# Two 128x512 elementwise steps of a quartered feed-forward pass, put on VectorE in place of GpSimd

## The chip, the cores and the metric

The kernel runs on one core of one Trainium2 chip. The metric is the device time of one launch in microseconds; of the kernel before there are three runs and one profiled execution. The core has five engines with a queue of their own each, taken in order: TensorE (PE in the profile, with its weight loads as PEld), VectorE (DVE), ScalarE (ACT), GpSimd (POOL) and SyncE (SP). Transfers are issued from such queues and then run on the DMA engines beside them.

## The reference

A bidirectional encoder of two layers on one sequence of 512 positions with 1024 features. Each layer is a half-step feed-forward, a mix of three kinds of attention, a second half-step feed-forward, and an embedding term that is gated. What matters here is the feed-forward, which stands four times in the program:

```
def swiglu(x, w_gate, w_up, w_down):
    return (jax.nn.silu(x @ w_gate) * (x @ w_up)) @ w_down
...
        h = h + 0.5 * swiglu(rms_norm(h, ffn1_norm[i]), ffn1_w_gate[i], ffn1_w_up[i], ffn1_w_down[i])
...
        h = h + 0.5 * swiglu(rms_norm(h, ffn2_norm[i]), ffn2_w_gate[i], ffn2_w_up[i], ffn2_w_down[i])
```

The inner width is 2816, so the gate and up products have 22 tiles of 128 columns each. All data is 32-bit float.

## The kernel before, in words

**Precision and passes.** Each operand of a matmul is split in a part hi of fewer bits (a cast on ScalarE, L101 for weights, L235 for data) and a rest lo (a subtraction on VectorE, L107 and L236). Each product runs in three passes on TensorE: hi by hi, lo by hi, hi by lo (mm3, L226 to L229, all recorded under L224). The weights are split in blocks of 1024 or, in the pass below, of 512 columns; at most two blocks ahead of the product that uses them, into three buffers of whi and wlo. Data is kept transposed, 128 features by 512 positions a tile.

**The stages.** The trace calls the four feed-forwards ffn10 (first one, layer 0), ffn20 (second one, layer 0), ffn11 and ffn21. In each, the 22 tiles go in 11 pairs. Pairs 0 and 1 are plain. Pairs 2 to 10 go in quarters: two halves of the features (z0 to z3 and z4 to z7) by the two tiles of the pair, over two halves A and B of the positions, with seven products of 128x256 instead of eight (class Quad, L462). One quad stands for the gate (g2 to g10), one for the up side (u2 to u10). A product is four mm3, so twelve matmuls with 256 columns. Products 1, 2, 5, 6, 3 and 7 of a pair's two quads come in turn, the gate's before the up's; product 4 is put off to the next pair, behind its products 1 and 2. After pairs 1, 3, 5, 7 and at the end stand groups of the down product (down_part, L546), whose results VectorE adds to h at L554; that frees their bank of the accumulator memory.

**A quad's operands.** Quad.load (L474) takes three tiles of raw weights, X and Y (128x1024) and Z (128x512). SyncE's queue loads them (L484 to L486), and GpSimd's queue then issues two transfers that add other weights to them in place: into Y's left half at L487 and into Z at L488. Two more sums are made on an engine: once the operand of product 1 has been split, X's left half gets Y's left half added (L496, on GpSimd), and once that of product 2 has been split, X's right half gets the new left half added (L498, on VectorE). The operands of products 6 and 3 are those two halves.

**A quad's results.** Product 1 is added up in a half bank called R, products 2, 5 and 3 in a bank called V. As partial sums are needed twice, ScalarE copies some out to tiles t1 and t2 (written ffn20g3t and so on): L517 after product 1, L519 after product 5, L521 after product 6. Product 3 goes on in the half bank that L519 reads, so it waits for this copy. VectorE finishes the first tile at L523 and the second from L525 on.

**The gate and its norm factor.** gate_half (L580) multiplies a finished gate tile by r, the norm factor of each position (L584 for the first tile, L586 and L587 for the two halves of the second), applies Silu on ScalarE (L588), and multiplies the result by r once more (L589, on GpSimd), so that the up side need not be scaled. up_half (L591) multiplies the up tile with it on VectorE (L594, or L596 and L597 for halves) and splits the product for the down matmuls (L235 and L236).

**What sets the order.** The program is written as a list of steps, with weights split ahead; a scheduler then places the instructions on the engines by its own estimates, and pins of program order hold only for the first pairs (L471 and L487). So an edit of one line can move others. GpSimd's queue holds, in a quartered stage, L487 and L488 (transfers), L496 and L589 (arithmetic), and in ffn10 also the transfers L333 that copy rows of a bias table. An L487 or L488 can be issued only when the plain load of its tile has landed, and what stands behind it on the queue waits as long.

Of the kernel before, what the change touches and what calls it, by code (L numbers as in the profile page):

```python
# [15 lines left out]
ALU = mybir.AluOpType  # L16
# [166 lines left out]
def encoder_kernel(ctx: ExitStack, tc: tile.TileContext, ins, out):  # L183
    nc = tc.nc
    L = ins["pT"].shape[0]
# [21 lines left out]
    def S(name, dt=F32):  # L207
        return sb.tile([P, 512], dt, tag="slot", name=name, bufs=SLOTS)
# [41 lines left out]
    t = S("one")  # L250
# [211 lines left out]
    class Quad:  # L462
# [29 lines left out]
        def took(self, i):  # L492

            L, R = slice(0, 512), slice(512, 1024)
            if i == 1:
                nc.gpsimd.tensor_tensor(self.X[:, L], self.X[:, L], self.Y[:, L], op=ALU.add)  # L496
            elif i == 2:
                nc.vector.tensor_add(self.X[:, R], self.X[:, R], self.X[:, L])  # L498

# [27 lines left out]
    def ffn(l, tag, prep, after, hooks={}):  # L527
# [52 lines left out]
        def gate_half(q, n):  # L580

            t, r = q.t[n], rb[0]
            if n == 0:
                nc.vector.tensor_mul(t, t, r)  # L584
            else:
                nc.vector.scalar_tensor_tensor(t[:, B], t[:, B], -1.0, r[:, B], op0=ALU.mult, op1=ALU.mult)  # L586
                nc.vector.scalar_tensor_tensor(t[:, A], q.R, -1.0, r[:, A], op0=ALU.mult, op1=ALU.mult)  # L587
            nc.scalar.activation(t, t, AF.Silu)  # L588
            nc.gpsimd.tensor_tensor(t, t, r, op=ALU.mult)  # L589

        def up_half(q, gq, n, f):  # L591
            t, g = q.t[n], gq.t[n]
# [15 lines left out]
        for p in range(PLAIN, PAIRS):  # L608
            G, U = [Quad(f"{name}{x}{p}", tag + "_w_" + w, p, prep) for x, w in (("g", "gate"), ("u", "up"))]
            for i in (1, 2):  # L610
                product(G, i)
                product(U, i)
            for fn in tail:
                fn()
            for i in (5, 6, 3, 7):
                product(G, i, (lambda G=G: gate_half(G, 0)) if i == 3 else lambda: None)
                product(U, i, (lambda G=G, U=U, p=p: up_half(U, G, 0, 2 * p)) if i == 3 else lambda: None)
            tail = [lambda G=G: product(G, 4, lambda: gate_half(G, 1)),
                    lambda G=G, U=U, p=p: product(U, 4, lambda: up_half(U, G, 1, 2 * p + 1))]
            if p in DOWN_AFTER:  # L620
                down(DOWN_AFTER[p])
# [904 lines left out]
```

## Time and profile before

| | us | 
|---|---|
| three runs | 2982.14, 2982.31, 2983.64 (median 2982.31) |
| the profiled execution, whole | 2985.1 |
| its span in the trace | 2983.3 |
| mean granted clock of TensorE | 0.997 of full |
| DMA | 141 GB/s over the span |

A row of the timeline gives the start, the duration, the engine, the line, the operation, the tile written and the tiles read, and in brackets the idle time of that engine ahead of it with what ended it. Instructions of an engine overlap a little, so the distance from one start to the next is shorter than the duration shown. For TensorE this matters most: a 256-column matmul is shown with 0.28 us while the next one starts 0.12 us later.

### The profile page before, as it was taken

To read this page: it belongs to the slowest core of one execution; us is meant where nothing else is said; L and a number is where in the kernel's file an instruction comes from. 1 tells how busy PE (TensorE), PEld (TensorE's weight loads), DVE (VectorE), ACT (ScalarE), POOL (GpSimd) and SP (SyncE) were. 2 spreads that over 40 slices of the span, in tenths; PEclk is the share of its full clock that TensorE was granted. 3 is DMA by queue.
4 is the path that set the end of the run, shared out by engine and by line. 5 is a ranking of instruction groups with operands and counts; after the bars stand their busy time and mean duration, and the time that the engine had idled before them with its cause. 6 is when DMAs were issued, how large, how long until landed. Compare 5 with 4: busy or idle time off the path is not lost. (4 is left out here: it accounts for less than half of the span.)

```text
span 2983.3 us, 45438 instructions
## 1 busy us (share of the span) xinstructions
PE 2920.9 (98%) x16812; PEld 2544.6 (85%) x16812; DVE 2079.9 (70%) x3515; ACT 1780.0 (60%) x3281; POOL 866.5 (29%) x1000
## 2 busy tenths in 40 slices
PE   8999999999999999999999999999999999999998
PEld 7989878888887888999889998788888888889996
DVE  7677776645787768767687776866467866676776
ACT  5444457767888855445454444677578888544443
POOL 1343103322333332322222331123223333322313
PEclk9999999999999999999999999999999999999999
DMA  6685335455555556553355645354555465655532
GB/s 209 160 253 157 120 123 134 100 134 138 142 128 122 139 147 196 158 142 106 120 161 150 178 106 171 95 121 111 134 135 149 103 149 132 185 161 147 154 96 85
DMA packets 133934, 421.45 MB, mean 141 GB/s; under 512 B 16174, under 2 KB 18542, under 8 KB 133712
## 3 DMA queue, kind: packets, MB, share of 16 engines
q0 software_dynamic: 53712, 156.01, 26.0%
q1 hardware_dynamic: 78272, 260.64, 25.7%
q8 instruction: 132, 2.16, 0.3%
q10 hardware_dynamic: 1728, 1.90, 0.2%
q14 instruction: 90, 0.74, 0.1%
HBM read 331.39 MB, written 18.94 MB: 117 GB/s over the span
## 5 line engine op out<-in xcount | busy, mean ns | idle before, releaser
L101 ACT CAST whi<-wraw 128x1024 fp32r<-128x1024 f32 x312 | 327.0, 1051 | 239.3 <-issue 55.0
L105 POOL DMA_DIRECT2D wlo<-wraw x146 | 126.8, 868 | 561.4 <-ACT wlo L104 470.8
L107 DVE TENSOR_TENSOR wlo<-wraw,whi 128x1024 fp32r<-128x1024 f32 x166 | 203.9, 1233 | 82.1 <-ACT whi L101 80.8
L104 ACT ACTIVATE wlo<-whi 128x1024 fp32r<-128x1024 f32 x146 | 154.9, 1061 | 2.1
L554 DVE SCALAR_TENSOR_TENSOR wo0h<-ffn11d,wo0h 128x512 f32<-128x512 f32 x48 | 33.0, 687 | 30.7 <-PE ffn11d L224 30.7
L554 DVE SCALAR_TENSOR_TENSOR wo0h<-ffn20d,wo0h 128x512 f32<-128x512 f32 x48 | 32.8, 687 | 29.5 <-PE ffn20d L224 29.5
L554 DVE SCALAR_TENSOR_TENSOR wo1h<-ffn21d,wo1h 128x512 f32<-128x512 f32 x48 | 32.8, 687 | 28.8 <-PE ffn21d L224 28.7
L554 DVE SCALAR_TENSOR_TENSOR x<-ffn10d,x 128x512 f32<-128x512 f32 x48 | 32.6, 686 | 27.4 <-PE ffn10d L224 27.3
L367 POOL TENSOR_TENSOR f_1sq<-f_1sq,f_1sq 128x512 f32<-128x512 f32 x14 | 21.4, 1528 | 49.3 <-ACT f_1sq L362 48.9
L917 ACT CAST m0kc<-m0kc 64x512 fp32r<-64x512 f32 x32 | 18.6, 582 | 15.0 <-PE m0kc L224 13.5
L917 ACT CAST m1kc<-m1kc 64x512 fp32r<-64x512 f32 x32 | 18.6, 582 | 14.9 <-PE m1kc L224 13.5
L870 DVE SCALAR_TENSOR_TENSOR m1qc<-m1qc,m1qc 64x512 fp32r<-64x512 f32 x16 | 11.0, 689 | 18.9 <-ACT m1qc L869 18.7
L870 DVE SCALAR_TENSOR_TENSOR m0qc<-m0qc,m0qc 64x512 fp32r<-64x512 f32 x16 | 11.0, 688 | 18.9 <-ACT m0qc L869 18.7
L1164 ACT ACT_TABLE_LOAD x16 | 20.5, 1283 | 0.3
L367 POOL TENSOR_TENSOR pg0sq<-pg0sq,pg0sq 128x512 f32<-128x512 f32 x7 | 10.6, 1513 | 23.9 <-ACT pg0sq L362 23.9
L367 POOL TENSOR_TENSOR pg1sq<-pg1sq,pg1sq 128x512 f32<-128x512 f32 x7 | 10.6, 1515 | 23.1 <-ACT pg1sq L362 23.1
L1348 POOL TENSOR_SCALAR out<-wo1h,small 128x512 f32<-128x512 f32 (+1 forms) x9 | 7.2, 799 | 32.5 <-DVE wo1h L1311 32.5
L938 DVE TENSOR_TENSOR m1vc<-m1vc,m1vc 128x256 fp32r<-128x256 f32 x16 | 6.4, 414 | 14.3 <-ACT m1vc L937 14.2
L938 DVE TENSOR_TENSOR m0vc<-m0vc,m0vc 128x256 fp32r<-128x256 f32 x16 | 6.4, 414 | 14.3 <-ACT m0vc L937 14.2
L869 ACT ACTIVATE m1qc<-m1qc 64x512 fp32r<-64x512 f32 x16 | 9.5, 592 | 10.4 <-PE m1qc L224 9.0
L869 ACT ACTIVATE m0qc<-m0qc 64x512 fp32r<-64x512 f32 x16 | 9.5, 592 | 10.4 <-PE m0qc L224 9.0
L224 PE MATMUL idle<-warm,ones 128*128 128x512 f32 x14 | 5.9, 603 | 8.5 <-DVE warm L254 8.5
(15134 smaller groups left out, 12591.9 us busy)
## 6 DMA issues: line engine op xcount, KB each, us to landing
wraw<-in_wall SPq DMA_DIRECT2D x312, 512.0 KB, 3.5
wlo<-wraw POOLq DMA_DIRECT2D x146, 512.0 KB, 4.6
copies_s<-bias_s POOLq DMA_DIRECT2D x16, 256.0 KB, 9.6
copies_d<-bias_d POOLq DMA_DIRECT2D x8, 512.0 KB, 10.7
h_dram<-x POOLq DMA_DIRECT2D x8, 256.0 KB, 2.7
pp_dram<-m0ppt POOLq DMA_DIRECT2D x8, 256.0 KB, 3.7
wo0h<-h_dram POOLq DMA_DIRECT2D x8, 256.0 KB, 7.1
ple0p<-pp_dram POOLq DMA_DIRECT2D x8, 256.0 KB, 4.4
```

The costliest lines, as they stand in the source:

```text
L101: pin(self.nc.scalar.copy(hi, raw))
L104: self.nc.scalar.activation(lo, hi.bitcast(F32), AF.Copy, scale=-1.0)
L105: self.nc.gpsimd.dma_start(lo.bitcast(F32), raw, accum_op=ALU.add)
L107: self.nc.vector.tensor_tensor(lo, raw, hi.bitcast(F32), op=ALU.subtract)
L367: self.engine.tensor_tensor(self.acc, self.acc, sq, op=ALU.add)
L554: nc.vector.scalar_tensor_tensor(h[d], ps, 0.5, h[d], op0=ALU.mult, op1=ALU.add)
L869: nc.scalar.activation(qs[e][own], ps[own], AF.Copy, scale=-0.125)
L870: nc.vector.scalar_tensor_tensor(qs[e][other], ps[own], -0.125, qs[e][own].bitcast(F32), op0=ALU.mult, op1=ALU.subtract)
L917: nc.scalar.copy(ks[e][r], ps[own])
L938: nc.vector.tensor_sub(t[:, 256:512], ps, t[:, 0:256].bitcast(F32))
L1164: nc.scalar.activation(r, ss, AF.Sqrt, bias=eps, scale=1.0 / P)
L1348: nc.gpsimd.tensor_scalar(gained[d][:, c], h[d][:, c], small[:, L * S_N + d:L * S_N + d + 1], 1.0, op0=ALU.mult, op1=ALU.mult)
```

## The change

Two lines move from GpSimd to VectorE. They compute the same; a quad has one L496 and a gate quad two L589, so 18 of each per feed-forward, 72 of each in the program.

```diff
@@ Quad.took
             if i == 1:
-                nc.gpsimd.tensor_tensor(self.X[:, L], self.X[:, L], self.Y[:, L], op=ALU.add)
+                nc.vector.tensor_add(self.X[:, L], self.X[:, L], self.Y[:, L])
             elif i == 2:
                 nc.vector.tensor_add(self.X[:, R], self.X[:, R], self.X[:, L])
@@ gate_half
             nc.scalar.activation(t, t, AF.Silu)
-            nc.gpsimd.tensor_tensor(t, t, r, op=ALU.mult)
+            nc.vector.tensor_mul(t, t, r)
```

How the built programs differ in order is shown at three places, all in ffn20 between pairs 2 and 3. VectorE first, from the split of pair 3's operands to the second up tile of pair 2. The wlo are the lo parts of pair 3's weights (g3x, u3x and g3z the raw tiles), ffn20g2t2 the second gate tile and ffn20u2t2 the second up tile of pair 2, f2_0r the norm factor:

```order
 L107 TENSOR_TENSOR wlo201_12168<-ffn20g3x_11767,whi201_12167 128x512
 L586 SCALAR_TENSOR_TENSOR ffn20g2t2_11869<-ffn20g2t2_11869,f2_0r_11456 128x256
 L107 TENSOR_TENSOR wlo201_12168<-ffn20u3x_11775,whi201_12167 128x512
+L587 SCALAR_TENSOR_TENSOR ffn20g2t2_11869<-ffn20g2R_11867,f2_0r_11456 128x256
 L107 TENSOR_TENSOR wlo202_12208<-ffn20g3x_11767,whi202_12207 128x512
 L107 TENSOR_TENSOR wlo202_12208<-ffn20u3x_11775,whi202_12207 128x512
-L587 SCALAR_TENSOR_TENSOR ffn20g2t2_11869<-ffn20g2R_11867,f2_0r_11456 128x256
+L589 TENSOR_TENSOR ffn20g2t2_11869<-ffn20g2t2_11869,f2_0r_11456 128x512
+L107 TENSOR_TENSOR wlo203_12240<-ffn20g3z_11769,whi203_12239 128x512
 L596 SCALAR_TENSOR_TENSOR ffn20u2t2_11885<-ffn20u2t2_11885,ffn20g2t2_11869 128x256
 L597 SCALAR_TENSOR_TENSOR ffn20u2t2_11885<-ffn20u2R_11883,ffn20g2t2_11869 128x256
-L107 TENSOR_TENSOR wlo203_12240<-ffn20g3z_11769,whi203_12239 128x512
```

L587 has moved ahead of two weight splits, L589 now stands on VectorE behind these two, and one more weight split stands ahead of L596.

GpSimd in the same stretch; the z and y tiles are those of pairs 4 and 5, L488 and L487 the transfers that add to them:

```order
 L488 DMA ffn20g4z_12046<-in_wall 128x512
-L589 TENSOR_TENSOR ffn20g2t1_11868<-ffn20g2t1_11868,f2_0r_11456 128x512
 L488 DMA ffn20u4z_12057<-in_wall 128x512
 L487 DMA ffn20g4y_12045<-in_wall 128x512
 L487 DMA ffn20u4y_12056<-in_wall 128x512
-L589 TENSOR_TENSOR ffn20g2t2_11869<-ffn20g2t2_11869,f2_0r_11456 128x512
 L488 DMA ffn20g5z_12311<-in_wall 128x512
```

Both L589 are gone from between the transfers, whose own order is unchanged.

ScalarE in the same stretch; ffn20u2t2 is the up tile just named, ffn20a5h its hi part, ffn20g3V and ffn20u3V the banks of pair 3's products 2, 5 and 3, and wraw172 a block of down weights:

```order
 L101 CAST whi203_12239<-ffn20u3z_11777 128x512
 L235 CAST ffn20a5h_12201<-ffn20u2t2_11885 128x512
+L101 CAST whi204_12271<-wraw172_11963 128x1024
 L519 COPY ffn20g3t2_12103<-ffn20g3V_12139 128x256
 L519 COPY ffn20u3t2_12119<-ffn20u3V_12152 128x256
-L101 CAST whi204_12271<-wraw172_11963 128x1024
```

The 1024-wide cast stood behind the two L519 copies and now stands ahead of them.

## Prediction

> **What bounds the kernel now.** I read the page's first part, then the windows over the quartered stretches, the waits of TensorE, and the timeline around single waits. The page gives the busy times, with the share of the span and the number of instructions:
>
> ```profile
> PE 2920.9 (98%) x16812; PEld 2544.6 (85%) x16812; DVE 2079.9 (70%) x3515; ACT 1780.0 (60%) x3281; POOL 866.5 (29%) x1000
> ```
>
> TensorE sets the time; the other engines matter only where they make it wait. The windows say how much that can be in the stages of the change. A row holds the window, its length, the busy time of PE, PEld, DVE, ACT and POOL, the clock and the DMA share. The long windows are the quartered stretches of ffn10, ffn20, ffn11 and ffn21, the short one a pair late in ffn20 with no down products in it:
>
> ```profile
> 85.00:345.00 260.00, 254.93 (x1766) 236.95 (x1765) 190.25 (x302) 120.15 (x220) 86.71 (x89) 1.00 0.59 169
> 1165.00:1430.00 265.00, 262.95 (x1832) 246.91 (x1831) 189.53 (x295) 122.15 (x225) 74.94 (x62) 1.00 0.50 139
> 1381.00:1401.00 20.00, 20.00 (x169) 20.00 (x168) 17.26 (x30) 11.75 (x23) 2.99 (x3) 1.00 0.22 72
> 1560.00:1830.00 270.00, 268.41 (x1858) 251.41 (x1857) 195.04 (x299) 124.14 (x229) 76.93 (x68) 1.00 0.52 143
> 2640.00:2880.00 240.00, 237.67 (x1709) 225.48 (x1709) 174.68 (x274) 113.25 (x214) 73.79 (x61) 1.00 0.51 141
> ```
>
> TensorE is idle for 5.07, 2.05, 1.59 and 2.33 us there, 11.04 together. No edit in these stages that leaves the matmuls alone can give much more. The list of TensorE's waits (who waits, for whom, us, times, longest) names nearly all of it:
>
> ```profile
> PE ffn21g3V L224 <- ACT ffn21g3t L519: 2.3, 1, 2.3
> PE ffn10d L224 <- DVE x L554: 2.3, 1, 2.3
> PE ffn10g3V L224 <- ACT ffn10g3t L519: 2.1, 1, 2.1
> PE ffn20g3V L224 <- ACT ffn20g3t L519: 2.1, 1, 2.1
> ...
> PE ffn11g3V L224 <- ACT ffn11g3t L519: 1.5, 1, 1.5
> ...
> PE ffn11u2V L224 <- DVE wlo L107: 1.0, 1, 1.0
> ```
>
> Four are the same wait, once in each feed-forward: product 3 of pair 3's gate waits for ScalarE's copy L519. I follow the one in ffn20 back through the engines. TensorE's rows:
>
> ```profile
> 1186.13 0.28 PE L224 MATMUL ffn20u3R<-f_0t643h,wlo 128*128 128x256 f32 x1
> 1186.25 0.28 PE L224 MATMUL ffn20u3R<-f_0t643l,whi 128*128 128x256 f32 x1
> 1188.58 0.39 PE L224 MATMUL ffn20g3V<-f_0z4h,whi 128*128 128x256 f32 x1 [2.05 <-ACT ffn20g3t L519]
> ```
>
> Matmuls follow at 0.12 us, so the next was due at 1186.37 and came 2.21 late: the idle time shown, and 0.16 that the 0.28 of a row hides. ScalarE, whose copy it waited for:
>
> ```profile
> 1182.05 0.63 ACT L588 ACTIVATE ffn20g2t<-ffn20g2t 128x512 f32<-128x512 f32 x1 [2.99 <-DVE ffn20g2t L587]
> ...
> 1187.63 0.62 ACT L235 CAST ffn20a5h<-ffn20u2t 128x512 fp32r<-128x512 f32 x1 [3.92 <-DVE ffn20u2t L597]
> 1188.16 0.37 ACT L519 COPY ffn20g3t<-ffn20g3V 128x256 f32<-128x256 f32 x1
> 1188.42 0.38 ACT L519 COPY ffn20u3t<-ffn20u3V 128x256 f32<-128x256 f32 x1
> 1188.69 1.06 ACT L101 CAST whi<-wraw 128x1024 fp32r<-128x1024 f32 x1
> ```
>
> The copy needs nothing from pair 2; it only stands behind L235, which waited 3.92 us for VectorE's L597. VectorE:
>
> ```profile
> 1180.40 0.68 DVE L107 TENSOR_TENSOR wlo<-ffn20g3x,whi 128x512 fp32r<-128x512 f32 x1
> 1181.00 0.68 DVE L107 TENSOR_TENSOR wlo<-ffn20u3x,whi 128x512 fp32r<-128x512 f32 x1
> 1181.61 0.41 DVE L587 SCALAR_TENSOR_TENSOR ffn20g2t<-ffn20g2R,f_0r 128x256 f32<-128x256 f32 x1
> 1186.84 0.42 DVE L596 SCALAR_TENSOR_TENSOR ffn20u2t<-ffn20u2t,ffn20g2t 128x256 f32<-128x256 f32 x1 [4.82 <-POOL ffn20g2t L589]
> ```
>
> VectorE stood 4.82 us for GpSimd's L589. And GpSimd:
>
> ```profile
> 1184.62 0.87 POOL L487 DMA_DIRECT2D ffn20u4y<-in_wall  x1 [2.64 <-DMA ffn20u4y<-in_wall]
> 1185.19 1.62 POOL L589 TENSOR_TENSOR ffn20g2t<-ffn20g2t,f_0r 128x512 f32<-128x512 f32 x1
> ```
>
> Silu's result was there at 1182.68 (1182.05 and 0.63), but L589 stood behind an L487, which waited for a load of pair 4's weights until 1184.62, and then took 1.62. So the wait comes of arithmetic in a queue of transfers, passed on through three queues.
>
> The wait in ffn10's down products (ffn10d) has the same root. GpSimd's queue and VectorE there, and the Silu in question:
>
> ```profile
> 174.50 0.63 ACT L588 ACTIVATE ffn10g5t<-ffn10g5t 128x512 f32<-128x512 f32 x1 [1.23 <-DVE ffn10g5t L584]
> ```
>
> ```profile
> 183.15 0.53 POOL L333 DMA_DIRECT2D copies_d<-bias_d  x1
> 183.69 1.30 POOL L589 TENSOR_TENSOR ffn10g5t<-ffn10g5t,f_0r 128x512 f32<-128x512 f32 x1
> ```
>
> ```profile
> 185.03 0.69 DVE L594 TENSOR_TENSOR ffn10u5t<-ffn10u5t,ffn10g5t 128x512 f32<-128x512 f32 x1 [8.49 <-POOL ffn10g5t L589]
> ```
>
> Silu was done at 175.13, but the bias table's copies stood ahead, and VectorE idled 8.49 us at L594, with the L554 that free TensorE's banks behind it.
>
> **The change part by part.** *L589 off GpSimd's queue, at the g3V waits.* Four waits go, 2.3+2.1+2.1+1.5 = 8.0 us shown and 4 x 0.16 hidden, 8.6 in all, unless something else is late next. What is next is the same chain without GpSimd, with starts spaced as in the rows above (0.60 for L107 and for L589 as its like in form, 0.34 for L596, 0.53 for L235, about 1.0 for the 1024-wide cast, which now stands ahead of L519). If L587 started no earlier: Silu's result at 1182.68, L589 at 1182.75, the L107 moved ahead of L596 at 1183.35, L596 at 1183.95, L597 at 1184.29 to 1184.71, L235 at 1184.75, the cast at 1185.28, L519 at 1186.3 to 1186.67, TensorE at 1186.72, which is 0.35 late. But L587 now stands ahead of two L107. If its input is there by then, Silu comes 1.2 earlier, L589 waits for the two L107 and starts at 1181.95, and all behind it comes 0.8 earlier: TensorE is served at 1185.92, 0.45 before it asks. As ScalarE had been idle for 2.99 us at that Silu, I take nothing late; the other end is 4 x 0.35 = 1.4 that stays.
>
> *L589 at ffn10d.* VectorE is free 8.49 us before L594 and now runs L589 there, so L594 and the L554 behind it come about 7.9 earlier; the wait of 2.3 goes with its hidden 0.16: 2.4.
>
> *The wait of ffn11u2V,* 1.0 and 0.16, is for VectorE's split of a weight. Its pair has had GpSimd's L496 in its midst and gets VectorE's. I can't tell how much goes: between 0 and 1.2, I take 0.6. Waits under half a us, such as remain at other weights, I leave as they are, old ones that go against new ones that come.
>
> *The work on VectorE.* 144 instructions at the 0.60 us from start to start seen between 1180.40 and 1181.00 are 86.4 us, 21.6 in each feed-forward. In ffn20's window VectorE goes from 189.5 of 265 (72%) to 211 (80%), and stays below TensorE. Part is given back, since GpSimd and VectorE slow each other. The two rows of such a meeting, then all 72 L498 of the program:
>
> ```profile
> 1357.00 1.75 POOL L496 TENSOR_TENSOR ffn20u9x<-ffn20u9x,ffn20u9y 128x512 f32<-128x512 f32 x1
> ```
>
> ```profile
> 1357.14 2.16 DVE L498 TENSOR_TENSOR ffn20g9x<-ffn20g9x 128x512 f32<-128x512 f32 x1
> ```
>
> ```profile
> 0.00:2983.30 2983.30, 71.95 (x72) 1.00 0.52 141
> ```
>
> L498 means 1.00 us (71.95 / 72) where a free 128x512 of its form takes 0.68: 0.32 x 72 = 23 us come back from this line if that goes, and VectorE's net load is then 63 us. [...]
>
> What VectorE's work costs TensorE depends on how far ahead the weights are. The shortest lead that I found is in the short window; the split, then TensorE's first use:
>
> ```profile
> 1384.37 0.68 DVE L107 TENSOR_TENSOR wlo<-ffn20g9y,whi 128x512 fp32r<-128x512 f32 x1
> ```
>
> ```profile
> 1386.48 0.28 PE L224 MATMUL ffn20g9R<-f_0t640h,whi 128*128 128x256 f32 x1
> ```
>
> At a rate of 0.60 the split was done by 1384.97, 1.5 us ahead. One or two added instructions (0.60 each) in front of a split are hidden by that; I take nothing, and pay for more in the first rival. L496 on VectorE can also wait at the head of its queue for the transfer into Y. On GpSimd it was released by one only once in 72, though VectorE may reach it sooner than GpSimd's queue did:
>
> ```profile
>   DMA ffn21u10y<-in_wall: 3.3, 1
> ```
>
> Where that happens, L498 and splits stand behind it; with the lead of 1.5 and one case in 72 I put it at nothing, its other end at 3.3 - 1.5 = 1.8. GpSimd's transfers, no longer behind arithmetic, start earlier where their tiles are in; TensorE waits for none of them here, so that gives nothing.
>
> *The sum.* 8.6 + 2.4 + 0.6 = 11.6 us off the profiled 2985.1 gives 2973.5. The median is 2.8 below that execution (2982.3 against 2985.1), so the median after would be 2970.7.
>
> **The rivals.** *VectorE becomes the bound (slower).* A pair takes TensorE 14 products x 12 matmuls x 0.12 = 20.16 us. VectorE's 17.26 in 20 is 17.4 in that time; four more instructions make 19.8, and if it stands at the head of its queue for Silu twice in a pair (0.63 and the way there and back, 0.8), 21.4: 1.2 over. Between down products lie three stretches of two pairs and one of three. Less the lead of 1.5 the former lose 0.9 each, the latter 2.1, so 4.8 a feed-forward and 19 in all; the g3V waits stay, as VectorE is late there too, and only the 2.4 of ffn10d is saved: 2982.3 + 19.2 - 2.4 = 2999. It decides from 20.16 us of VectorE time and unhidden waits per pair on. For it speaks the 86% of the short window. Against it: if L498 gets its 0.32 back twice a pair, 21.4 becomes 20.8, and the excess in a two-pair stretch (1.2) is below the lead; and VectorE has idled in the waits for GpSimd that now go. [...]
>
> *A new wait in place of the old (no change).* Product 3 is late again because L519 stands behind L235 and now behind the 1024-wide cast too. If VectorE reaches L597 two instructions (1.2 us) later than in the chain without L587's advance, TensorE is 0.35 + 1.2 = 1.55 late in each feed-forward: 6.2 of the 8.6 stay, and 2.4 + 2.4 = 4.8 are gained: 2977.5. It decides once L597 ends after 1184.4 on ffn20's clock. For it: the cast of 1.0 us that moved ahead, and a margin of only 0.45. Against it: ScalarE's idle 2.99 and 3.92 there, and the earlier L587.
>
> **How the numbers follow.** The forecast gets 0.74, the new wait 0.17, VectorE as the bound 0.09. A measurement of this kernel can tell about 0.2%, 6 us, from no change; the forecast is beyond it, the new wait within it, the bound slower: 0.74, 0.17, 0.09. The low end has all of ffn11u2V (0.6 more), 1.5 for the spread of the runs, and 1.6 for pauses under 0.16 us that a row of TensorE hides: 2967.0. The high end has the new wait at its worst, all 8.6 left and 2.4 gained, 2979.9, and 1.1 of the runs' spread: 2981.0. VectorE as the bound is left out.
>
> **What would show it.** In the profile after, the list of TensorE's waits should hold no g3V on L519 and no ffn10d on L554; VectorE's L594 and L596 should show no idle time put down to GpSimd; L498 should mean 0.68; VectorE's busy time in ffn20's window should be about 205 (211 less 18 x 0.32). The forecast is wrong if TensorE waits for wlo of L107 in the stretches of two and three pairs (VectorE as the bound, worst before the last down products), or for L519 with the 1024-wide cast just ahead of it (the new wait).

## The result, and the profile after

| | before | after |
|---|---|---|
| six runs, median (us) | 2983.40 (2982.14 to 2985.95) | 2968.93 (2968.43 to 2970.88) |
| ratio | 1 | 0.9948, 95% interval 0.9938 to 0.9959 |
| span of the profiled execution (us) | 2983.3 | 2967.0 |
| four feed-forwards, first matmul to last, summed (us) | 1401.0 | 1387.5 |

The forecast was 2970.7 in 2967.0 to 2981.0, and faster. The gain is 14.5 us by medians and 16.3 by the two profiled spans, of which 13.5 lie in the feed-forwards. The page's busy times, and the windows over the same four stretches as before (each moved to its new place), the third row ffn20's short one:

```profile
PE 2917.5 (98%) x16812; PEld 2543.3 (86%) x16812; DVE 2118.4 (71%) x3659; ACT 1786.1 (60%) x3281; POOL 652.2 (22%) x856
```

```profile
80.00:340.00 260.00, 260.00 (x1811) 242.61 (x1810) 201.89 (x341) 125.11 (x228) 39.82 (x57) 1.00 0.60 174
1155.00:1420.00 265.00, 265.00 (x1849) 249.08 (x1848) 201.80 (x329) 125.56 (x228) 24.36 (x28) 1.00 0.51 141
1370.00:1390.00 20.00, 20.00 (x169) 20.00 (x168) 16.34 (x29) 11.77 (x22) 0.00 (x0) 1.00 0.23 79
1547.00:1817.00 270.00, 270.00 (x1874) 253.37 (x1873) 204.53 (x334) 126.69 (x232) 27.56 (x34) 1.00 0.52 144
2624.00:2864.00 240.00, 240.00 (x1731) 228.06 (x1731) 186.37 (x309) 116.50 (x218) 24.31 (x28) 1.00 0.53 143
```

TensorE's busy time equals the window's length in every row: the 11.04 us of idle time that the rows before showed are gone. (A pause that the 0.28 us of a row covers doesn't show in them; one place with such pauses is left in ffn11, see below.) In TensorE's list of waits one row is left for the feed-forwards, at the start of a stage, far from the change:

```profile
PE ffn11g L224 <- ACT f_1z6h L408: 0.2, 1, 0.2
```

The wait that the prediction followed, in ffn20, now looks so on TensorE (last matmul of product 6, first of product 3):

```profile
1177.92 0.28 PE L224 MATMUL ffn20u3R<-f_0t643l,whi 128*128 128x256 f32 x1
1178.04 0.28 PE L224 MATMUL ffn20g3V<-f_0z4h,whi 128*128 128x256 f32 x1
```

so on ScalarE,

```profile
1171.50 0.63 ACT L588 ACTIVATE ffn20g2t<-ffn20g2t 128x512 f32<-128x512 f32 x1 [0.71 <-DVE ffn20g2t L587]
...
1174.58 0.62 ACT L235 CAST ffn20a5h<-ffn20u2t 128x512 fp32r<-128x512 f32 x1 [0.90 <-DVE ffn20u2t L597]
1175.36 1.05 ACT L101 CAST whi<-wraw 128x1024 fp32r<-128x1024 f32 x1 [0.17 <-DMA ffn20g5x<-in_wall]
1176.32 0.37 ACT L519 COPY ffn20g3t<-ffn20g3V 128x256 f32<-128x256 f32 x1
```

and so on VectorE:

```profile
1171.04 0.42 DVE L587 SCALAR_TENSOR_TENSOR ffn20g2t<-ffn20g2R,f_0r 128x256 f32<-128x256 f32 x1
1171.38 0.68 DVE L107 TENSOR_TENSOR wlo<-ffn20g3x,whi 128x512 fp32r<-128x512 f32 x1
1171.98 0.69 DVE L107 TENSOR_TENSOR wlo<-ffn20u3x,whi 128x512 fp32r<-128x512 f32 x1
1172.59 0.68 DVE L589 TENSOR_TENSOR ffn20g2t<-ffn20g2t,f_0r 128x512 f32<-128x512 f32 x1
1173.19 0.69 DVE L107 TENSOR_TENSOR wlo<-ffn20g3z,whi 128x512 fp32r<-128x512 f32 x1
1173.79 0.42 DVE L596 SCALAR_TENSOR_TENSOR ffn20u2t<-ffn20u2t,ffn20g2t 128x256 f32<-128x256 f32 x1
1174.13 0.41 DVE L597 SCALAR_TENSOR_TENSOR ffn20u2t<-ffn20u2R,ffn20g2t 128x256 f32<-128x256 f32 x1
```

The matmuls follow at 0.12 us. VectorE goes through the whole chain without a pause; where it stood 4.82 us for GpSimd there is no bracket. L519 ends at 1176.69 and TensorE asks at 1178.04: 1.35 us to spare, with the 1024-wide cast ahead of the copy.

VectorE's busy time grew by only 38.5 us (2118.4 less 2079.9), though the two lines take 86.4 there at 0.60 from start to start (96.6 by the durations of their rows, which overlap a little). What came back is seen in lines that the change did not touch. First all L498 after; then all L107, before and after:

```profile
0.00:2967.00 2967.00, 48.11 (x72) 1.00 0.53 142
```

```profile
0.00:2967.00 2967.00, 554.80 (x670) 1.00 0.52 141
```

```profile
0.00:2967.00 2967.00, 532.81 (x670) 1.00 0.53 142
```

L498 means 0.67 us where it was 1.00 (23.8 us back), and the weight splits took another 22.0 less.

### The profile page after: what moved, and what is told of

The parts are those of the page before. It is cut to its first block, busy times and chain, and to the rows that moved or that the text cites. A ratio compares the mean times of both kernels' runs of the same rounds, so it can differ in the third digit from the quotient of the medians.

```text
span 2967.0 us, 45265 instructions
## 1 busy us (share of the span) xinstructions
PE 2917.5 (98%) x16812; PEld 2543.3 (86%) x16812; DVE 2118.4 (71%) x3659; ACT 1786.1 (60%) x3281; POOL 652.2 (22%) x856
## 4 chain that ended last, share of the span: by engine, by line
PE 86%; ACT 5%; DVE 5%; issue 2%; DMA 1%; POOL 1%; DVEq 0%; ACTq 0%; SPq 0%; POOLq 0%
PE ffn21d L224 4%; PE ffn20d L224 4%; PE ffn10d L224 4%; PE ffn11d L224 4%; PE ple L224 3%; PE wo L224 2%; PE m1ga L224 1%; PE m0ga L224 1%; PE m1qb L224 1%; PE m1qc L224 1%; PE m0qc L224 1%; PE m0qb L224 1%; PE m0vc L224 1%; PE m1vc L224 1%; PE m0gb L224 1%
## 5 line engine op out<-in xcount | busy, mean ns | idle before, releaser
L107 DVE TENSOR_TENSOR wlo<-wraw,whi 128x1024 fp32r<-128x1024 f32 x166 | 204.1, 1233 | 107.2 <-ACT whi L101 98.8
L917 ACT CAST m1kc<-m1kc 64x512 fp32r<-64x512 f32 x32 | 18.6, 582 | 15.0 <-PE m1kc L224 13.5
L917 ACT CAST m0kc<-m0kc 64x512 fp32r<-64x512 f32 x32 | 18.6, 582 | 15.0 <-PE m0kc L224 13.5
L870 DVE SCALAR_TENSOR_TENSOR m1qc<-m1qc,m1qc 64x512 fp32r<-64x512 f32 x16 | 11.0, 689 | 18.9 <-ACT m1qc L869 18.8
L870 DVE SCALAR_TENSOR_TENSOR m0qc<-m0qc,m0qc 64x512 fp32r<-64x512 f32 x16 | 11.0, 688 | 18.9 <-ACT m0qc L869 18.7
## 6 DMA issues: line engine op xcount, KB each, us to landing
copies_d<-bias_d POOLq DMA_DIRECT2D x8, 512.0 KB, 10.7
```

The lines of the kernel that those rows point to most:

```text
L107: self.nc.vector.tensor_tensor(lo, raw, hi.bitcast(F32), op=ALU.subtract)
L870: nc.vector.scalar_tensor_tensor(qs[e][other], ps[own], -0.125, qs[e][own].bitcast(F32), op0=ALU.mult, op1=ALU.subtract)
L917: nc.scalar.copy(ks[e][r], ps[own])
```

## The experiments

Eight kernels, each with a profile. Beside the time stands the length of the four feed-forwards, which the profile gives to a tenth of a microsecond, while runs of the kernel before spread from 2980.5 to 2991.6 us on the chips of these runs. "Half clock" is what of that length the matmuls lost in stretches in which TensorE ran at half its clock (granted 0.51 in e2, 0.50 in d8), 0.21 us from start to start instead of 0.12 (last section); the kernel before has no such stretch in its feed-forwards. The ratios are to runs of the kernel before on the chip of the experiment (median 2985.49 us for e1 to e5, 2984.54 for the others), not to the 2983.40 of the first row.

| kernel | median (us) | ratio to before (95%) | feed-forwards (us) | half clock | against before |
|---|---|---|---|---|---|
| before | 2983.40 | | 1401.0 | | |
| after | 2968.93 | 0.9948 (0.9938 to 0.9959) | 1387.5 | | -13.5 |
| e1_norm_only | 2974.57 | 0.9964 (0.9950 to 0.9978) | 1391.5 | | -9.5 |
| e2_sum_only | 2977.25 | 0.9974 (0.9964 to 0.9984) | 1396.1 | 1.5 | -5.0 |
| e3_five | 2973.67 | 0.9960 (0.9947 to 0.9972) | 1390.8 | | -10.3 |
| e5_queue_order | 2973.97 | 0.9960 (0.9948 to 0.9973) | 1391.8 | | -9.2 |
| e7_sum_and_order | 2971.60 | 0.9956 (0.9939 to 0.9973) | 1389.6 | 1.5 | -11.4 |
| d4_load | 2970.73 | 0.9954 (0.9939 to 0.9969) | 1389.3 | 1.5 | -11.8 |
| d8_load | 2989.15 | 1.0016 (1.0006 to 1.0025) | 1410.3 | 7.0 | +9.2 |
| d12_load | 3028.15 | 1.0146 (1.0131 to 1.0161) | 1447.0 | 10.7 | +45.9 |

The theory under test: arithmetic queued behind transfers on GpSimd made the waits. Its rivals: contention between GpSimd and VectorE made them; GpSimd's slowness as an engine made them.

**e1_norm_only.** One line of the two.

```diff
-            nc.gpsimd.tensor_tensor(t, t, r, op=ALU.mult)
+            nc.vector.tensor_mul(t, t, r)
```

> All 72 L589 on VectorE, all 72 L496 still on GpSimd. Theory (arithmetic queued behind transfers on GpSimd): the four g3V waits (8.6 us), ffn10d (2.4) and the two g10V waits (1.0) go, so about 12 us under the kernel before, within 2 us of the changed kernel; L498 still means near 1.00 us. Rival, port contention between GpSimd and VectorE makes the gain: it would split by the work moved, L496 117.5 and L589 107.8 us of GpSimd time, so about 6 to 7 us here and L498's mean decides.

TensorE's waits in the feed-forwards, from 0.5 us on:

```profile
PE ffn11u2V L224 <- DVE wlo L107: 1.0, 1, 1.0
PE ffn10u2R L224 <- DVE wlo L107: 0.8, 1, 0.8
PE ffn10g10V L224 <- ACT ffn10g10t L519: 0.6, 1, 0.6
PE ffn11g10V L224 <- ACT ffn11g10t L519: 0.5, 1, 0.5
```

All g3V waits and ffn10d are gone, as the theory has it. L498, though, means 0.77 (55.38 us in 72) where near 1.00 was expected: most of its stretch, too, went with L589 (0.23 of 0.33 us). That the contention is at a port, as the rival has it, no run shows; they show it as the longer L498. And the gain is 9.5, between the theory's 12 and the rival's 6 to 7: u2V and the two g10V stay, and a u2R of 0.8 and a g9V of 0.3 are new, from causes that weren't followed. The g10V I had given to L589; like u2V they are gone in e2, where L496 alone moves. So e1 doesn't decide against contention by itself; e3 and e5 do.

**e2_sum_only.** The other line alone.

```diff
-                nc.gpsimd.tensor_tensor(self.X[:, L], self.X[:, L], self.Y[:, L], op=ALU.add)
+                nc.vector.tensor_add(self.X[:, L], self.X[:, L], self.Y[:, L])
```

> All 72 L496 on VectorE, all 72 L589 still on GpSimd. Theory: the g3V waits and ffn10d stay, 2 us or less are gained (the wait of ffn11u2V and the like), though L498 falls to about 0.68 us. Rival, port contention: about 7 us are gained.

TensorE's waits in the feed-forwards, from 0.5 us on:

```profile
PE ffn10g3V L224 <- ACT ffn10g3t L519: 2.5, 1, 2.5
PE ffn20g3V L224 <- ACT ffn20g3t L519: 1.2, 1, 1.2
PE ffn21g3V L224 <- ACT ffn21g3t L519: 0.7, 1, 0.7
PE ffn10d L224 <- DVE x L554: 0.6, 1, 0.6
PE ffn11g3V L224 <- ACT ffn11g3t L519: 0.6, 1, 0.6
```

The waits stay, as expected, but three of the g3V and ffn10d are much shorter, u2V and g10V are gone, and 5.0 us are gained (6.5 without the half clock) instead of 2 or less. By size alone the rival's 7 is nearer than the theory's 2, so e2 doesn't decide between them; that the waits would stay and grow shorter neither side had. At the g3V waits the reason is one link further back. GpSimd in this kernel:

```profile
1182.43 0.86 POOL L487 DMA_DIRECT2D ffn20u4y<-in_wall  x1 [2.85 <-DMA ffn20u4y<-in_wall]
1182.99 1.62 POOL L589 TENSOR_TENSOR ffn20g2t<-ffn20g2t,f_0r 128x512 f32<-128x512 f32 x1
```

The L487 waits for a plain load, and that load waits for a buffer: it goes into the tile of pair 2's Y, free once VectorE has split its last half. The split and SyncE's load, before, then in this kernel:

```profile
1178.26 0.68 DVE L107 TENSOR_TENSOR wlo<-ffn20u2y,whi 128x512 fp32r<-128x512 f32 x1
```

```profile
1178.97 0.33 SPq L484 DMA_DIRECT2D ffn20u4y<-in_wall  x1
```

```profile
1175.91 0.68 DVE L107 TENSOR_TENSOR wlo<-ffn20u2y,whi 128x512 fp32r<-128x512 f32 x1
```

```profile
1176.62 0.33 SPq L484 DMA_DIRECT2D ffn20u4y<-in_wall  x1
```

Both come 2.35 us earlier; TensorE was 1.34 earlier there by then, so the chain gained 1.0 on it. With L496 on VectorE this split moves up in its queue by one place, 0.6 of the 1.0; that it is also held up less by contention (L498 means 0.86 here) is likely but not separated. So L496 was not idle in the g3V waits: VectorE's lateness came back to VectorE through SyncE's load and GpSimd's queue.

**e3_five.** Five of the 144 instructions.

```diff
-            nc.gpsimd.tensor_tensor(t, t, r, op=ALU.mult)
+            (nc.vector if (q.p, n) == (PLAIN, 1) or (name, q.p, n) == ("ffn10", 5, 0) else nc.gpsimd).tensor_tensor(t, t, r, op=ALU.mult)
```

> Only five of the 144 instructions move to VectorE: L589 of pair 2's second gate tile in each of the four feed-forwards, and of pair 5's first gate tile in ffn10. Theory: 8.6 + 2.4 = 11 us of the 13.4 that the quartered stages gained come from these five, so 11 us under the kernel before, the g10V waits stay. Rival, VectorE's or GpSimd's load and contention in general: 5/144 of the gain, under 1 us.

All four g3V waits and ffn10d are gone, with the orders of TensorE and ScalarE as before. The feed-forwards are 10.3 us shorter, against 11 expected: five instructions give three quarters of the 13.5. u2V (1.0 us) and ffn11's g10V (0.8) stay. L498 still means 1.01 (72.81 in 72), so less contention is no part of these 10.3.

**e5_queue_order.** Nothing leaves GpSimd. Pair 2's second L589 is put ahead of pair 4's two L487, by issuing these behind it in the program and pinning that order.

```diff
-            self.pin(nc.gpsimd.dma_start(Y[:, L], wall[m][:, R], accum_op=ALU.add))
+            late(self, PLAIN + 2, lambda: nc.gpsimd.dma_start(Y[:, L], wall[m][:, R], accum_op=ALU.add))
...
-            nc.gpsimd.tensor_tensor(t, t, r, op=ALU.mult)
+            first(tc, nc.gpsimd.tensor_tensor(t, t, r, op=ALU.mult), steps, (q.p, n) == (PLAIN, 1), PLAIN + 2)
...
+def late(quad, pair, add):
+    if quad.p == pair:
+        quad.late = add
+    else:
+        quad.pin(add())
+
+
+def first(tc, ins, steps, here, pair):
+    if here:
+        tc.keep_in_program_order(ins)
+        for kind, what, _ in steps:
+            if kind == "product" and what[0].p == pair and what[1] == 1:
+                tc.keep_in_program_order(what[0].late())
```

> All arithmetic stays on GpSimd; only the order of GpSimd's queue changes, in one place of each feed-forward: pair 2's second L589 goes ahead of the two L487 of pair 4. VectorE's and ScalarE's orders stay those of before. Theory (the queue): in ffn20's clock L589 runs from 1182.75 to 1184.4, L596 starts at 1184.45, L597 ends at 1185.2, L235 starts at 1185.25, L519 ends at 1186.15, before the 1186.37 at which TensorE asks: the four g3V waits (8.6 us) go, ffn10d stays, 8 us gained. Rival, GpSimd's slowness as an engine (1.6 us against 0.6): most of the waits stay, under 2 us gained.

GpSimd at that place, and ScalarE's copy:

```profile
1179.47 1.29 POOL L589 TENSOR_TENSOR ffn20g2t<-ffn20g2t,f_0r 128x512 f32<-128x512 f32 x1 [8.62 <-ACT ffn20g2t L588]
1180.71 0.87 POOL L487 DMA_DIRECT2D ffn20g4y<-in_wall  x1
```

```profile
1182.12 0.37 ACT L519 COPY ffn20g3t<-ffn20g3V 128x256 f32<-128x256 f32 x1
```

L589 now waits for Silu and for nothing else, and the copy is done at 1182.49, before TensorE asks (1183.06). All four g3V waits are gone and 9.2 us are gained with the slow engine and the contention as before (L498 means 0.98) and with the orders of all four other engines the same, instruction for instruction. That rules out both rivals for these waits. Half of ffn10d went too (2.3 to 1.2): L589 comes 4.6 us earlier there and TensorE 3.2; what brought L589 forward by the rest wasn't followed.

**e7_sum_and_order.** e5 with L496 on VectorE.

```diff
-                nc.gpsimd.tensor_tensor(self.X[:, L], self.X[:, L], self.Y[:, L], op=ALU.add)
+                nc.vector.tensor_add(self.X[:, L], self.X[:, L], self.Y[:, L])
```

> L496 on VectorE as in the changed kernel, but all 72 L589 stay on GpSimd, with pair 2's second one put ahead of the two L487 of pair 4 as in e5_queue_order. Theory (the order of GpSimd's queue, not the engine of L589, makes the g3V waits; L496 on VectorE makes those of ffn11u2V and g10V go): no g3V, u2V or g10V wait; about 1 us is left at ffn10d, where L589 still stands behind bias copies; the four feed-forwards together 12 us shorter than before, 1 to 1.5 longer than in the changed kernel. Rival (L589 must leave GpSimd): the g3V waits come back in part, 9 us shorter or less.

No wait of the list is left but the 0.2 of ffn11g that the changed kernel has too; ffn20, ffn11 and ffn21 are as long as in the changed kernel to 0.1 us, and ffn10 is 2.1 longer, 1.5 of it half clock. So L589 need not leave GpSimd at all; it must not stand behind the transfers. ffn10d went further than expected. What moving L496 adds to e5 (12.9 less 9.2 us, without the half clock) may come of VectorE's other order or of less contention (L498 means 0.86); no run separates the two.

**d4_load, d8_load, d12_load.** The changed kernel with two, four or six maxima of the dead up tile behind each split, for VectorE alone (shown for two; nothing waits for them):

```diff
-            a[f] = split(t, f"{name}a{f}")
+            a[f] = split(t, f"{name}a{f}"); [nc.vector.tensor_max(t, t, t) for _ in range(2)]
```

> The changed kernel with VectorE work added that nothing waits for: after each split of an up tile, two in-place maxima of that dead tile (128x512), 4 a pair, 144 in all. The short window of the changed kernel shows VectorE at 16.34 of 20, so 16.5 in a pair's 20.16; with 4 x 0.60 that is 18.9. Theory (a pair of 20.16 on TensorE is the bound, VectorE's load is free below it): no more than 1 us over the changed kernel. Rival (every addition to VectorE's queue delays TensorE somewhere): 144 x 0.60 = 86 us of work cost several us.

> As d4_load with four maxima each, 8 a pair, 288 in all: VectorE 21.3 in a pair's 20.16, 1.1 over. Theory: with a lead of 1.5 the stretches of two pairs lose 0.7 each, that of three 1.8, 3.9 a feed-forward and 16 us in all over the changed kernel, at waits for wlo of L107 at the ends of the stretches. Rival (VectorE's load never matters, only the order of queues): within 1 us of the changed kernel.

> As d4_load with six maxima each, 12 a pair, 432 in all: VectorE 23.7 in a pair's 20.16, 3.5 over. Theory: stretches of two pairs lose 5.5 each, that of three 9.0, 25.5 a feed-forward and about 100 us in all over the changed kernel. Rival: the scheduler spreads the work into the down products, where VectorE has room, and the cost is under half of that.

Windows of ffn20's last stretch (three pairs, between down products) with d4 and d8, with d8 also of 14 us late in it, then of a stretch of two pairs and of the last with d12; in the changed kernel the stretch of two pairs is 40.3 us long and the last one 60.5:

```profile
1333.20:1393.70 60.50, 60.50 (x506) 60.50 (x505) 55.41 (x96) 35.14 (x69) 5.23 (x6) 1.00 0.41 107
```

```profile
1341.30:1405.80 64.50, 63.01 (x506) 62.27 (x505) 59.24 (x103) 35.27 (x69) 5.23 (x6) 0.97 0.37 93
1375.00:1389.00 14.00, 12.59 (x99) 11.86 (x97) 14.00 (x26) 7.64 (x17) 0.00 (x0) 1.00 0.22 56
```

```profile
1229.40:1271.50 42.10, 40.98 (x337) 40.48 (x336) 38.44 (x67) 22.52 (x43) 5.23 (x6) 1.00 0.60 163
1357.20:1425.90 68.70, 64.07 (x505) 62.31 (x504) 64.35 (x113) 35.08 (x69) 5.23 (x6) 0.98 0.39 100
```

With d4, 144 more instructions (98.5 us on VectorE) cost nothing: the feed-forwards are 1.8 longer than in the changed kernel, 1.5 of it half clock. With d8 they are 22.8 longer, 15.8 without the half clock, where 16 was expected. In the 14 us late in the stretch VectorE is busy throughout and TensorE for 12.59, so there VectorE is the bound. The waits stand near the ends of stretches, as expected, and mostly of the last one in each feed-forward, but the largest are for VectorE's L525, which finishes a tile, and not for wlo of L107:

```profile
PE ffn10g9R L224 <- DVE ffn10g9t L525: 1.5, 1, 1.5
PE ffn11g9R L224 <- DVE ffn11g9t L525: 1.5, 1, 1.5
```

The split between stretches was off, though: in ffn20 the last one loses 4.0 us (1.5 of it half clock) and those of two pairs nothing. With d12 the feed-forwards are 59.5 longer, 48.8 without the half clock, about half of the 100 expected: a two-pair stretch loses 1.8 instead of 5.5, the last 8.2 (1.4 of it half clock) instead of 9.0. Of the 24 maxima that two pairs bring, 9 run beside down products (of the 16 with d8, 4), so the rival there, that work is spread into them, has the reason; its "under half" holds only without the half clock. The border agrees with the prediction's 20.16: it lies between 18.9 and 21.3 us of VectorE work per pair, and nothing between these two was run.

## Why the prediction was right, step by step

**The g3V waits,** 8.6 forecast: TensorE's lead over the kernel before grows by 2.4, 2.3, 1.7 and 2.6 us at the four places, 9.0 in all; 0.4 of it is the matmul behind each wait, which came 0.1 late too. The scheduler also moved some of TensorE's own matmuls in the changed kernel (around pair 3 in ffn10 and pair 2 in ffn11), but e3 and e5 keep TensorE's order and lose the same four waits. The cause stands, by e5 more narrowly than I had put it: not that L589 ran on GpSimd, but its place there. I also stopped a link too early: the load that GpSimd waited for was itself waiting for VectorE (e2).

**What would be late next:** nothing, and the spare time is 1.35 us, not 0.45. L587 came 2.24 us earlier against TensorE (1181.61 and 1171.04, TensorE's due times 1186.37 and 1178.04) where I took 1.2, as VectorE's earlier work moved up too.

**ffn10d,** 2.4 forecast: 2.5 by TensorE's lead. **ffn11u2V,** 0.6 in 0 to 1.2: 0.7. Its wait is gone from the list, but VectorE's split is still late there (it ends at 1543.62), and three matmuls of later products, which the scheduler put ahead, follow with pauses too short for the list:

```profile
1542.92 0.28 PE L224 MATMUL ffn11u2V<-f_1z4h,whi 128*128 128x256 f32 x1
1543.04 0.28 PE L224 MATMUL ffn11g2V<-f_1t570h,whi 128*128 128x256 f32 x1
1543.26 0.38 PE L224 MATMUL ffn11g2R<-f_1t640h,whi 128*128 128x256 f32 x1
1543.78 0.39 PE L224 MATMUL ffn11u2R<-f_1t640h,whi 128*128 128x256 f32 x1
1544.00 0.28 PE L224 MATMUL ffn11u2V<-f_1z4h,wlo 128*128 128x256 f32 x1
```

From 1542.92 to 1544.00 four matmuls go where nine have room at 0.12. The gain is L496's: the wait is there in e1, e3 and e5, and gone in e2 and e7, which have this order of TensorE too.

**Waits under half a us,** set at nothing against new ones: this term was mis-sized. ffn10g10V, ffn11g10V and ffn10g2R gave 0.7, 0.4 and 0.3, together 1.4, and no new ones came that the list shows. 9.0 + 2.5 + 0.7 + 1.4 is 13.6, the 13.5 measured but for rounding, against 11.6.

**VectorE's load.** The net was forecast at 63 us, with L498's stretch given back; it is 38.5, because the weight splits (L107) gave back as much as L498, which I had left out. So ffn20's window shows 201.8, not 205. **VectorE as the bound** was given 0.09 and an arithmetic that d8 bears out in its sum but not in its parts, so that agreement is partly luck. VectorE's wait for Silu is also less than half of what I took, 0.7 us once in a pair instead of 0.8 twice,

```profile
DVE ffn20g3t L589 <- ACT ffn20g3t L588: 0.7, 1, 0.7
```

for the second gate tile only, in 30 of 36 pairs; ahead of L589 for the first tile, other work of VectorE covers the time that Silu takes. **The new wait** behind the 1024-wide cast did not come, by 1.35 us.

**The time.** The forecast median was 1.8 us too high, and that it came so near is in part luck. The stages gave 1.9 more than the sum. The rest of the change, outside these stages, gave 2.8; and the forecast took off 2.8 because the profiled execution before was that much above its median, while the one after (2968.80) is 0.1 below its own. These two cancel. The two profiled spans differ by 16.3; of what is over 13.5, 1.5 is a stretch at half clock in layer 0's mix that the kernel before had there and the changed one had not, and 0.5 a shorter wait of m0va on L850 there; the rest, 0.8, lies at the two ends. None of that is in a stage that the change touches, and the cause of the m0va difference stays open.

## What to carry to other kernels

A queue that holds transfers which wait for their buffers is a bad place for arithmetic that someone else waits for; look at what stands ahead of an instruction on its queue, not at how fast its engine is: here 9.2 us came of L589's place alone, with L589 still on GpSimd (1.29 us in ffn20, against 0.68 on VectorE). Moving the order, or five instructions of 144, can give most of what a whole move gives (9.2 and 10.3 of 13.5 us), and the profile names the five. Before giving an engine more work, count its time per unit of the bound engine's work: here 16.5 of 20.16 us a pair, and work up to 18.9 was all but free (1.8 us longer, 1.5 of it half clock) while 21.3 was not (22.8 longer, 7.0 of it half clock).

## What the runs showed of the hardware that was not expected

In some places a wait of about 2 us cost TensorE more than itself. In the kernel before, layer 0's mix (m0qb), the window over a wait of 1.88 us and the one behind it; the clock is the third column from the end:

```profile
912.00:914.20 2.20, 0.37 (x2) 0.00 (x0) 0.58 (x3) 2.20 (x9) 1.00 (x2) 1.00 1.02 190
914.80:918.20 3.40, 3.40 (x10) 2.61 (x9) 1.98 (x3) 2.99 (x6) 2.13 (x4) 0.51 1.05 261
```

For 3.4 us the granted clock is 0.51, matmuls follow at 0.43 us instead of 0.23, and 1.5 us are lost. The same wait in the changed kernel was followed by full clock (1.00 from 907.6 to 911.0 us); over the ten profiles, this wait and its like in layer 1 (m1qb, 1.9 us too) were followed by half clock 13 times in 20 (in layer 1 of the kernel before 0.50 from 2389.6 to 2392.8, of the changed one 0.50 from 2375.3 to 2378.7). In e2 it came behind ffn10's g3V wait of 2.5 us (0.51 from 104.9 to 108.3); behind the g3V waits of the kernel before, of 1.5 to 2.3 us, it didn't come in the profiled execution (in ffn20, 1.00 from 1188.6 to 1192.0). It also came without a wait: in e7 and the three load kernels it came in ffn10, at 150 to 154 us, with TensorE never idle in the 10 us ahead, behind six matmuls of only 33 rows (bv, L321, 2.75 us), which the changed kernel has too, without it (1.00 from 150 to 154). What decides stays open. Five runs each of e1, e3 and e5 spread over 0.8 to 2.4 us, thirteen of the kernel before on the same chip over 11.1; but four of e7, which has none of the g3V waits either, spread over 5.0, so that fewer such waits make the difference isn't shown.
